# First layer's low weight parts by an adding transfer, with the norm weights moved to the activations

## The chip, the cores and the metric

The kernel runs on one NeuronCore of one Trainium2 chip. The metric is the device time of one execution in microseconds (us); lower is better. Engines are named as in the profile: PE (TensorE matmul) and PEld (its weight loads), DVE (VectorE), ACT (ScalarE), POOL (GpSimd), SP (SyncE, which here only issues transfers).

## What is computed

The reference is a two-layer trunk on a sequence of 512 positions with 1024 features, all in float32:

```python
h = rms_norm(x, norm_g)                       # (512, 1024)
zxbcdt = h @ w_in                             # (1024, 6176): z, x/B/C, dt
xbc = silu(causal_depthwise_conv(xbc, conv_w, conv_b))
y = ssd_chunked_scan(xs * dt, a * dt, bm, cm) + d_skip * xs
y = gated_group_rms_norm(y, z, gate_norm_g)   # silu(z) gate, 8 groups, times g
x = x + y @ w_out                             # (2048, 1024)
k, v = shared_kv(x, kv_norm_g, w_kv)          # second layer: differential attention
x = diff_attention_layer(x, k, v, b_norm_g, b_w_in, ...)
return rms_norm(x, final_norm_g)
```

The first layer is everything up to the second `x =` line. Its two weights are `w_in` and `w_out`; `norm_g` scales the rows of `w_in`, `gate_norm_g` the rows of `w_out`.

## The kernel before

**Split products.** Every dense product is made of three matmuls in the reduced float32 format (float32r). A weight block is split into a high part (the value rounded to float32r) and a low part (what is left), an activation likewise, and `mm3` adds high x high, high x low and low x high into one PSUM bank. So a weight block is of use only when both of its parts are there.

**Segments.** The weights come as a list of segments (`segs`), each 1 MB: 128 partitions x 2048 values. The first layer has 32: `z0_0, z0_1, g0_0, g0_1, g1_0, ...` in the order `z0 g0 g1 z1 g2 g3 z2 g4 o0 g5 z3 g6 g7 o1 o2 o3`, two halves each; `z` and `g` are pieces of `w_in`, `o` of `w_out`. They are numbered 0 to 31 in that order. PE spends 48 matmuls of 512 columns on each.

**Loading and splitting** (`load`, from line 139). One transfer on SP's queue brings the segment into a tile `raw` (two buffers). `split` then makes the tiles `whi` and `wlo` (two buffers each) in four quarters of 128x512: `head` is an ACT instruction that multiplies by the norm weights (one value per partition, `gains`) and rounds; `rest` is a DVE instruction `raw * gain - whi`. Segment 0 is special: its quarters come in four transfers of their own, between those of the transposed input `x_t`, and the first matmuls begin with the first quarter. `split` is a function inside `load` that is called after `load` has returned, and it names its tiles with the variable `i`; in `load(0)` that variable is also the counter of a `for i in range(2, 4)` loop. So the tiles of segment 0 are called `whi3` and `wlo3`.

**What sets the order.** `use(seg)` fetches two segments ahead of the one in use. In the first layer PE's order is the program's; the other engines' instructions are put in order by a scheduler that works with its own estimate of durations, so each engine is a fixed queue once the program is built. POOL makes the decay tiles (`dec`: a subtraction and a masking per head, lines 613 to 616), the state products (`xe`, `hst`) and sums (`dx`). The convolution, the gate and the norm of each group are on DVE and ACT.

**Activations.** `split_x` makes the high part `a_hi` (ACT) and low part `a_lo` (DVE) of the transposed input, without any norm weight; the row factor of the norm comes in later. At the end of each group's scan the normed `y` is transposed into PSUM and split into `yh` and `yl`.

Of the kernel before, what the change touches and what calls it, by code (L numbers as in the profile page):

```python
# [17 lines left out]
P = 128  # L18
# [38 lines left out]
C_GA, C_GK, C_GB, C_GG, C_SG, C_DTB, C_AL, C_CB, C_CW = 0, 8, 16, 24, 40, 41, 42, 43, 75  # L57
# [24 lines left out]
def trunk(ctx, tc, x, x_t, par, w_dt, w_in, w_out, w_kvqg, w_bo, d_skip, lam_qk, fin_g, out):  # L82
    nc = tc.nc
    V, A, T = (Ordered(tc, e) for e in (nc.vector, nc.scalar, nc.tensor))
    GP = nc.gpsimd
# [13 lines left out]
    def ss_bank(name):  # L99
        turns[0] += 1  # L100
        tag = "mm" if turns[0] % turns[1] >= 3 else "ss"
        return psum.tile([P, 512], F32, tag=tag, name=name, bufs=3 if tag == "ss" else 4)
# [8 lines left out]
    segs = []  # L111
# [4 lines left out]
    prm = const.tile([P, C_CB], F32, name="prm")  # L116
# [8 lines left out]
    def source(seg):  # L125
        kind, a, b = seg
        if kind == "z":
            return w_in[a * 6 + b], [prm[:, C_GA + 4 * b + i:C_GA + 4 * b + i + 1] for i in range(4)]
        if kind == "g":
            return w_in[(a // 2) * 6 + 2 + (a % 2) * 2 + b], [prm[:, C_GA + 4 * b + i:C_GA + 4 * b + i + 1] for i in range(4)]  # L130
        if kind == "o":
            return w_out[a * 2 + b], [prm[:, C_GG + 4 * a + i:C_GG + 4 * a + i + 1] for i in range(4)]
        if kind in "bc":
            return w_bo[a], None
        name = f"v{a}" if kind == "v" else a
        at = C_GK if kind in "vk" else C_GB
        ks = range(4 * b, 4 * b + 4) if kind == "v" else range(8)
        return w_kvqg[BLOCKS.index((name, b))], [prm[:, at + i:at + i + 1] for i in ks]
# [5 lines left out]
    def load(i):  # L144

        seg = segs[i]
        src, gains = source(seg)
        nk = 8 if seg[0] in "kqt" else 4
        w = 2048 // nk
        raw = begun[i] if i in begun else wp.tile([P, nk, w], F32, tag="raw", name=f"raw{i}", bufs=2)  # L150
        fetched[0] += 1

        def split():

            pool, tags = (bp, ("dec", "dec")) if seg == ("o", 3, 1) else (wp, ("whi", "wlo"))
            if pool is bp:
                hi, lo = (pool.tile([P, N_DEC], F32R, tag=tag, name=f"{n}{i}", bufs=2)[:, 0:2048].rearrange("p (k n) -> p k n", k=nk)
                          for n, tag in zip(("whi", "wlo"), tags))
            else:
                hi, lo = (pool.tile([P, nk, w], F32R, tag=tag, name=f"{n}{i}", bufs=2) for n, tag in zip(("whi", "wlo"), tags))  # L160
            ready[seg] = (hi, lo)

            def head(k):
                if gains:
                    A.activation(hi[:, k, :], raw[:, k, :], AF.Copy, scale=gains[k])
                else:
                    A.copy(hi[:, k, :], raw[:, k, :])

            def rest(k):
                if gains:  # L170
                    V.scalar_tensor_tensor(out=lo[:, k, :], in0=raw[:, k, :], scalar=gains[k],
                                           in1=hi[:, k, :].bitcast(F32), op0=ALU.mult, op1=ALU.subtract)
                else:
                    V.tensor_tensor(out=lo[:, k, :], in0=raw[:, k, :], in1=hi[:, k, :].bitcast(F32), op=ALU.subtract)

            return [(head, rest, k) for k in range(nk)]

        if i == 0:

            nc.sync.dma_start(raw[:, 0, :], src[:, 0:w])  # L180
            for n in range(2):
                nc.sync.dma_start(xt[0][:, 0, n * 256:(n + 1) * 256], x_t[:, 0, n * 256:(n + 1) * 256])
            nc.sync.dma_start(raw[:, 1, :], src[:, w:2 * w])
            for n in range(2):
                nc.sync.dma_start(xt[0][:, 1, n * 256:(n + 1) * 256], x_t[:, 1, n * 256:(n + 1) * 256])
            for k in range(2, 4):
                nc.sync.dma_start(raw[:, k, :], src[:, k * w:(k + 1) * w])
                nc.sync.dma_start(xt[1][:, k - 2, :], x_t[:, k, :])

            nxt, (src1, _) = wp.tile([P, nk, w], F32, tag="raw", name="raw1", bufs=2), source(segs[1])  # L190
            begun[1] = nxt
            for i in range(2, 4):
                nc.sync.dma_start(xt[i], x_t[:, 2 * i:2 * i + 2, :])
                nc.sync.dma_start(nxt[:, 2 * i - 4:2 * i - 2, :].rearrange("p k n -> p (k n)"), src1[:, (2 * i - 4) * w:(2 * i - 2) * w])
            nc.sync.dma_start(prc[:], par[:, C_CB:N_PAR])
        elif i not in begun:
            nc.sync.dma_start(raw.rearrange("p k n -> p (k n)"), src)
        return split
# [162 lines left out]
    def new_h(tag):  # L361
        return [res.tile([P, KD, S], F32R, tag=f"hT_{i}", name=f"{tag}_{i}") for i in ("hi", "lo")]
# [9 lines left out]
    hh, hl = new_h("a")  # L372
    sctx = ExitStack()
    sm = sctx.enter_context(tc.tile_pool(name="setup", bufs=1))
# [22 lines left out]
    xt = [bp2.tile([P, 2, S], F32, tag="yl", name=f"xt{i}", bufs=4) for i in range(4)]  # L397

    def split_x(k, n=slice(0, S)):
        A.copy(hh[:, k, n], xt[k // 2][:, k % 2, n])  # L400
        V.tensor_tensor(out=hl[:, k, n], in0=xt[k // 2][:, k % 2, n], in1=hh[:, k, n].bitcast(F32), op=ALU.subtract)


    begin = small.tile([P, 1], F32, name="begin", bufs=1)
# [5 lines left out]
    for k in range(4):  # L410
        lay(first[k])
        for n in (slice(0, 256), slice(256, S)) if k < 2 else (slice(0, S),):
            split_x(k, n)
# [5 lines left out]
    for k in range(4, KD):  # L419
        split_x(k)  # L420
# [22 lines left out]
    pre = sm.tile([P, P], F32, name="pre")  # L443
# [4 lines left out]
    e1 = sm.tile([P, P], F32, name="e1")  # L448
# [3 lines left out]
    q1 = sm.tile([P, P], F32, name="q1")  # L452
# [3 lines left out]
    q2 = sm.tile([P, P], F32, name="q2")  # L456
# [3 lines left out]
    for m in (15, 13, 11, 9, 7, 5, 3):  # L460
        V.scalar_tensor_tensor(out=pl, in0=pl, scalar=2.0 / m, in1=q2, op0=ALU.add, op1=ALU.mult)
    V.scalar_tensor_tensor(out=pl, in0=pl, scalar=2.0, in1=q1, op0=ALU.add, op1=ALU.mult)
    dtp = sm.tile([P, P], F32, name="dtp")
    V.scalar_tensor_tensor(out=dtp, in0=pre, scalar=0.0, in1=pl, op0=ALU.max, op1=ALU.add)
    ea = sm.tile([P, 1], F32, name="ea")
    A.activation(ea, prm[:, C_AL:C_AL + 1], AF.Exp)
    adt = sm.tile([P, P], F32, name="adt")
    V.tensor_scalar(out=adt, in0=dtp, scalar1=ea, scalar2=-1.0, op0=ALU.mult, op1=ALU.mult)
    ones = sm.tile([P, P], F32, name="ones")
    GP.memset(ones, 1.0)  # L470
    acs = sm.tile([P, P], F32, name="acs")
    V.tensor_tensor_scan(out=acs, data0=ones, data1=adt, initial=0.0, op0=ALU.mult, op1=ALU.add)
    acs_d = tc.dram_tile([H, NQ, P], F32, name="acs_d")
    for c in range(NQ):
        nc.sync.dma_start(acs_d[:, c, :], acs[c * H:(c + 1) * H, :])
    toe = sm.tile([P, P], F32, name="toe")
    A.activation(toe, acs, AF.Exp, scale=-1.0, bias=acs[:, P - 1:P])
    dsk = const.tile([P, H], F32, name="dsk")
    nc.sync.dma_start(dsk[:], d_skip.partition_broadcast(P))
# [143 lines left out]
    def ssd(g):  # L623
# [7 lines left out]
        for c in range(NQ):  # L631
            cs = slice(c * P, (c + 1) * P)
# [10 lines left out]
        for j in range(2):  # L643
# [6 lines left out]
            with tc.issue_after(next_b.ins) if next_b else ExitStack():  # L650
                V.tensor_tensor(out=xdt[:, :, 2 * j:2 * j + 2, :], in0=pv, in1=dt_tok[:, :, h2].unsqueeze(3).to_broadcast([P, NQ, 2, HD]), op=ALU.mult)
                V.tensor_tensor(out=dx[:, :, 2 * j:2 * j + 2, :], in0=pv,
                                in1=dsk[:, h2].unsqueeze(1).unsqueeze(3).to_broadcast([P, NQ, 2, HD]), op=ALU.mult)
# [42 lines left out]
        for c in (2, 3):  # L696
            T.matmul(po2[:, (c - 2) * 256:(c - 1) * 256], lhsT=cc[:, c * P:(c + 1) * P], rhs=hsf[:, c - 1], start=True, stop=True)
        V.tensor_tensor(out=tmp[:, 1], in0=po1[:, 256:512].rearrange("p (h e) -> p h e", e=HD),
                        in1=eacs_tok[:, 1, hs].unsqueeze(2).to_broadcast([P, R, HD]), op=ALU.mult)
        V.tensor_tensor(out=tmp[:, 2:4], in0=po2.rearrange("p (c h e) -> p c h e", h=R, e=HD),  # L700
                        in1=eacs_tok[:, 2:4, hs].unsqueeze(3).to_broadcast([P, 2, R, HD]), op=ALU.mult)
# [15 lines left out]
        yh = bp2.tile([P, 2, S], F32R, tag="yh", name=f"yh{g}", bufs=4)  # L717
        yl = bp2.tile([P, 2, S], F32R, tag="yl", name=f"yl{g}", bufs=4)
        pyt = [ss_bank(f"pyt{g}_{j}") for j in range(2)]

        n = 2 if g == G - 1 else NQ
        for j, a in [(j, a) for a in range(0, NQ, n) for j in range(2)]:
            if not j:
                yield f"y{a}"
            for c in range(a, a + n):
                T.transpose(pyt[j][:, c * P:(c + 1) * P], tm[:, c, j * P:(j + 1) * P], ident)
            cs = slice(a * P, (a + n) * P)
            A.copy(yh[:, j, cs], pyt[j][:, cs])
            V.tensor_tensor(out=yl[:, j, cs], in0=pyt[j][:, cs], in1=yh[:, j, cs].bitcast(F32), op=ALU.subtract)
        yT[g] = (yh, yl)  # L730

    T.on = True
# [4 lines left out]
    hh, hl = new_h("b")  # L737
# [284 lines left out]
    def half(t, n):  # L1022
        hs = slice(n * 512, (n + 1) * 512)
        return x_tok[:, t, hs], fg[:, hs], ot[t][:, hs], out[t * P:(t + 1) * P, hs]
# [123 lines left out]
    y, f, o, dst = half(3, 0)  # L1148
# [8 lines left out]
    y, f, o, dst = half(3, 1)  # L1157
# [68 lines left out]
```

## Time and profile before

| | |
|---|---|
| median of 3 runs | 708.61 us (708.11 to 708.91) |
| the profiled execution: its own time | 709.16 us |
| its span in the trace | 707.4 us |
| granted TensorE clock, mean over the span | 0.998 |
| busy: PE, PEld | 697.1 us (99%), 579.8 us (82%) |
| busy: DVE, ACT, POOL | 519.5 us (73%), 426.2 us (60%), 113.4 us (16%) |
| read from HBM | 68.02 MB |

The span runs from the first to the last instruction of the trace, and the execution's own time is 1.76 us longer. Busy shares are of the span. The first layer's matmuls run from about 6 us to about 427 us, and what follows is the second layer.

### The profile page before, as it was taken

How to read it: one execution, taken by the hardware profiler on the slowest of the kernel's cores; microseconds unless marked ns; L12 is line 12 of the kernel's file. 1: busy time of each engine (PE TensorE's matmuls, PEld its weight loads, DVE VectorE, ACT ScalarE, POOL GpSimd, SP SyncE). 2: the span in 40 equal slices, each digit the busy share in tenths (PEclk: the TensorE clock that was granted, in tenths of full speed). 3: DMA queues.
4: the chain of work that ended last, by engine and by line, in shares of the span. 5: the costliest groups of instructions: out<-in, count | busy, mean ns of one | idle time of the engine just before them, and what ended most of it. 6: DMA issues, size and time to landing. Idle time of an engine off the chain costs nothing.

```text
span 707.4 us, 10489 instructions
## 1 busy us (share of the span) xinstructions
PE 697.1 (99%) x3838; PEld 579.8 (82%) x3838; DVE 519.5 (73%) x1181; ACT 426.2 (60%) x931; POOL 113.4 (16%) x158
## 2 busy tenths in 40 slices
PE   8999999999999999999999999999999999999996
PEld 7787888887788888888888888888888888888884
DVE  5479975888579669568996846457778657788786
ACT  6748673664653636637636357567777567765556
POOL 0008422402406025041110101000000000000002
PEclk9999999999999999999999999999999999999999
DMA  8643313233033331331122311313112221113003
GB/s 296 253 151 152 120 59 149 91 120 120 38 142 120 100 137 62 111 128 60 60 76 105 120 60 49 136 62 113 67 60 79 86 75 61 68 56 116 31 1 119
DMA packets 13492, 70.85 MB, mean 100 GB/s; under 512 B 1793, under 2 KB 3329, under 8 KB 6017
## 3 DMA queue, kind: packets, MB, share of 16 engines
q1 hardware_dynamic: 13008, 69.90, 27.0%
q8 instruction: 30, 0.49, 0.3%
q10 hardware_dynamic: 432, 0.28, 0.1%
q14 instruction: 22, 0.17, 0.1%
HBM read 68.02 MB, written 2.16 MB: 99 GB/s over the span
## 4 chain that ended last, share of the span: by engine, by line
PE 88%; DVE 4%; DMA 3%; ACT 2%; issue 1%; POOL 1%; SPq 0%; ACTq 0%; POOLq 0%
PE pg L73 23%; PE po L73 16%; PE pt L73 8%; PE pz L73 7%; PE pq L73 6%; PE pk L73 6%; PE pv L73 6%; PE pb L73 3%; DMA raw<-in_w_in 3%; PE sc L73 3%; PE pyd L73 2%; PE pc L73 2%; DVE wlo L73 1%; PE pcb L73 1%; PE psA L73 1%
## 5 line engine op out<-in xcount | busy, mean ns | idle before, releaser
L73 DVE SCALAR_TENSOR_TENSOR wlo<-raw,prm,whi 128x512 fp32r<-128x512 f32 (+1 forms) x240 | 148.7, 669 | 49.2 <-ACT whi L73 47.5
L73 ACT ACTIVATE whi<-raw,prm 128x512 fp32r<-128x512 f32 (+1 forms) x240 | 133.6, 628 | 51.2 <-issue 13.0
L73 PE MATMUL pg<-a_hi,whi 128*128 128x512 f32 x256 | 103.1, 403 | 0.8 <-DVE xc L73 0.4
L73 PE MATMUL pg<-a_hi,wlo 128*128 128x512 f32 x256 | 100.3, 392 | 0.1
L73 PE MATMUL pg<-a_lo,whi 128*128 128x512 f32 x256 | 99.8, 390 | 0.0
L73 DVE SCALAR_TENSOR_TENSOR xc<-pg,prc,xc 128x511 f32<-128x511 f32 (+2 forms) x96 | 69.6, 742 | 6.5 <-ACT xc L73 6.0
L73 PEld LDWEIGHTS pg<-a_hi,wlo 128*128 128x128 f32 x256 | 48.0, 188 | 11.5 <-DVE wlo L73 1.5
L73 PEld LDWEIGHTS pg<-a_hi,whi 128*128 128x128 f32 x256 | 48.1, 188 | 11.2 <-ACT xc L73 0.8
L73 PEld LDWEIGHTS pg<-a_lo,whi 128*128 128x128 f32 x256 | 48.1, 188 | 9.3
L73 PE MATMUL po<-whi,yh 128*128 128x512 f32 x128 | 51.7, 404 | 0.1
L73 PE MATMUL pz<-whi,a_hi 128*128 128x512 f32 x128 | 49.8, 398 | 1.3 <-DVE xc L73 0.7
L73 PE MATMUL po<-whi,yl 128*128 128x512 f32 x128 | 50.1, 391 | 0.0
L73 PE MATMUL po<-wlo,yh 128*128 128x512 f32 x128 | 50.0, 390 | 0.0
L73 PE MATMUL pz<-whi,a_lo 128*128 128x512 f32 x128 | 48.9, 390 | 0.0
L73 PE MATMUL pz<-wlo,a_hi 128*128 128x512 f32 x128 | 48.9, 389 | 0.0
L1031 POOL TENSOR_TENSOR ot<-x_tok,fg 128x512 f32<-128x512 f32 x4 | 5.0, 1284 | 248.9 <-DVE x_tok L73 248.9
L73 ACT ACTIVATE s<-s,mx 128x128 f32<-128x128 f32 (+3 forms) x64 | 35.6, 557 | 10.2 <-DVE mx L73 10.1
L73 DVE CUSTOM_DVE_ANT_0 s<-sc,bias 128x128 f32<-128x128 f32 (+3 forms) x64 | 29.3, 488 | 15.3 <-PE sc L73 14.8
L73 ACT ACTIVATE xc<-pg,prc 128x512 f32<-128x512 f32 x32 | 24.8, 775 | 25.2 <-DVE pg L73 19.6
L656 POOL TENSOR_TENSOR xe<-xdt,tok 128x256 f32<-128x256 f32 x24 | 14.1, 613 | 159.8 <-DVE xdt L73 159.8
L73 ACT ACTIVATE xc<-xc 128x512 f32<-128x512 f32 x32 | 20.0, 629 | 28.0 <-DVE xc L73 24.1
L73 ACT ACT_TABLE_LOAD x23 | 29.5, 1283 | 10.2 <-DVE xc L73 8.7
(238 smaller groups left out, 1629.8 us busy)
## 6 DMA issues: line engine op xcount, KB each, us to landing
raw<-in_w_in SPq DMA_DIRECT2D x22, 1024.0 KB, 4.9
raw<-in_w_kvqg SPq DMA_DIRECT2D x16, 1024.0 KB, 4.8
dec<-acs_d SPq DMA_DIRECT2D x8, 1024.0 KB, 5.4
raw<-in_w_out SPq DMA_DIRECT2D x8, 1024.0 KB, 4.8
raw<-in_w_bo SPq DMA_DIRECT2D x4, 1024.0 KB, 4.8
x_tok<-in_x SPq DMA_DIRECT2D x4, 512.0 KB, 8.9
out<-ot SPq DMA_DIRECT2D x6, 256.0 KB, 2.1
raw<-in_w_in SPq DMA_DIRECT2D x4, 256.0 KB, 5.0
```

Source lines behind the costliest of these rows:

```text
L73: i = op(*args, **kw)
L656: GP.tensor_tensor(out=xe[:, c], in0=xdt[:, c], in1=toe_tok[:, c, hs].unsqueeze(2).to_broadcast([P, R, HD]), op=ALU.mult)
L1031: GP.tensor_tensor(out=o, in0=y, in1=f, op=ALU.mult)
```

## The change

- For the segments of the first layer whose index satisfies a condition (`added`, below), `rest` is no longer a DVE instruction. POOL writes `-whi` into `wlo`, quarter by quarter, and after the fourth quarter POOL issues one transfer that reads the whole segment from HBM a second time and adds it onto `wlo`.
- The norm weights of the first layer leave the weights: `head` is a plain rounding copy there, `split_x` multiplies the input by `norm_g`, and the split of `y` multiplies by `gate_norm_g`, each in the same instruction as before.
- `whi` and `wlo` have three buffers instead of two. To make room, four small tiles of the setup share others' space (`dtp` is `pre`, `adt` is `q2`, `acs` is `e1`, `toe` is `q1`), and the space for descriptors of POOL's transfers is set to 1024 bytes.

```diff
-            return w_in[a * 6 + b], [prm[:, C_GA + 4 * b + i:C_GA + 4 * b + i + 1] for i in range(4)]
+            return w_in[a * 6 + b], None
...
+            added = seg[0] in "zgo" and 1 < i < segs.index(("o", 3, 0))
...
-                hi, lo = (pool.tile([P, nk, w], F32R, tag=tag, name=f"{n}{i}", bufs=2) for n, tag in zip(("whi", "wlo"), tags))
+                hi, lo = (pool.tile([P, nk, w], F32R, tag=tag, name=f"{n}{i}", bufs=3) for n, tag in zip(("whi", "wlo"), tags))
...
             def rest(k):
-                if gains:
+                if added:
+                    GP.tensor_scalar(out=lo[:, k, :], in0=hi[:, k, :].bitcast(F32), scalar1=-1.0, scalar2=None, op0=ALU.mult)
+                    if k == nk - 1:
+                        GP.dma_start(lo.rearrange("p k n -> p (k n)"), src, accum_op=ALU.add)
+                elif gains:
...
     def split_x(k, n=slice(0, S)):
-        A.copy(hh[:, k, n], xt[k // 2][:, k % 2, n])
-        V.tensor_tensor(out=hl[:, k, n], in0=xt[k // 2][:, k % 2, n], in1=hh[:, k, n].bitcast(F32), op=ALU.subtract)
+        ga = prm[:, C_GA + k:C_GA + k + 1]
+        A.activation(hh[:, k, n], xt[k // 2][:, k % 2, n], AF.Copy, scale=ga)
+        V.scalar_tensor_tensor(out=hl[:, k, n], in0=xt[k // 2][:, k % 2, n], scalar=ga, in1=hh[:, k, n].bitcast(F32),
+                               op0=ALU.mult, op1=ALU.subtract)
...
-            A.copy(yh[:, j, cs], pyt[j][:, cs])
-            V.tensor_tensor(out=yl[:, j, cs], in0=pyt[j][:, cs], in1=yh[:, j, cs].bitcast(F32), op=ALU.subtract)
+            gg = prm[:, C_GG + 2 * g + j:C_GG + 2 * g + j + 1]
+            A.activation(yh[:, j, cs], pyt[j][:, cs], AF.Copy, scale=gg)
+            V.scalar_tensor_tensor(out=yl[:, j, cs], in0=pyt[j][:, cs], scalar=gg, in1=yh[:, j, cs].bitcast(F32),
+                                   op0=ALU.mult, op1=ALU.subtract)
```

The condition reads `i` when `split` runs. For segment 0 that value is 3, left there by the loop in `load(0)`, so `added` holds for segment 0 too; it does not hold for segment 1 nor for 30 and 31. In all, 29 segments are concerned.

POOL's queue at the start of the program, before. `ident` is the unit matrix for transposes, `adiag` belongs to the input's norm, `dec0` and `dec1` are the decay tiles of the first two groups:

```order
masks.py:199 AFFINE_SELECT ident_74<-ident_74 128x128
L337 MEMSET adiag_253 128x128
L339 TENSOR_TENSOR adiag_253<-ident_74,ar_col_239 128x128 x4
L613 COPY dec0_543<-dec0_543 128x8
L615 TENSOR_TENSOR dec0_543<-dec0_543,tok_434 128x512 x4
L616 AFFINE_SELECT dec0_543<-dec0_543 128x512 x2
L613 COPY dec1_562<-dec1_562 128x8
L616 AFFINE_SELECT dec0_543<-dec0_543 128x512 x2
L615 TENSOR_TENSOR dec1_562<-dec1_562,tok_434 128x512 x4
```

The same place now, where `wlo3_134` is the low part of segment 0:

```order
masks.py:199 AFFINE_SELECT ident_74<-ident_74 128x128
L172 TENSOR_SCALAR wlo3_134<-whi3_133 128x512 x4
L174 DMA wlo3_134<-in_w_in 128x2048
L342 MEMSET adiag_254 128x128
L344 TENSOR_TENSOR adiag_254<-ident_74,ar_col_240 128x128 x4
L172 TENSOR_SCALAR wlo2_346<-whi2_345 128x512 x4
L174 DMA wlo2_346<-in_w_in 128x2048
L172 TENSOR_SCALAR wlo3_359<-whi3_358 128x512 x4
L174 DMA wlo3_359<-in_w_in 128x2048
L172 TENSOR_SCALAR wlo4_438<-whi4_437 128x512 x4
```

The low part of segment 0 is now four negations and one transfer of the whole 1 MB at the head of this queue.

PE's queue at the same place, before. The `pz0` banks take the products of segment 0:

```order
L73 MATMUL pz0_2_137<-whi3_133,a_hi_80 128x512
L73 MATMUL pz0_3_138<-whi3_133,a_hi_80 128x512
L73 MATMUL pz0_0_135<-wlo3_134,a_hi_80 128x512
L73 MATMUL pz0_1_136<-wlo3_134,a_hi_80 128x512
L73 MATMUL pz0_2_137<-wlo3_134,a_hi_80 128x512
```

And now:

```order
L73 MATMUL pz0_2_137<-whi3_133,a_hi_80 128x512
L73 MATMUL pz0_3_138<-whi3_133,a_hi_80 128x512
L73 MATMUL pz0_0_135<-wlo3_134,a_hi_80 128x512
L73 MATMUL pz0_0_135<-whi3_133,a_lo_81 128x512
L73 MATMUL pz0_1_136<-wlo3_134,a_hi_80 128x512
```

In both, the fifth matmul of segment 0 is the first that reads the low part, and 43 more of that segment stand behind it.

POOL's queue a little later, now. `wlo5_503` is the low part of segment 5, the second half of `g1`; the `dec` work is the same as before the change, in another place:

```order
L620 COPY dec0_544<-dec0_544 128x8
L620 COPY dec1_563<-dec1_563 128x8
L174 DMA wlo4_438<-in_w_in 128x2048
L172 TENSOR_SCALAR wlo5_503<-whi5_502 128x512 x4
L622 TENSOR_TENSOR dec0_544<-dec0_544,tok_433 128x512 x4
L622 TENSOR_TENSOR dec1_563<-dec1_563,tok_433 128x512 x4
L174 DMA wlo5_503<-in_w_in 128x2048
```

The transfer of segment 5 stands behind both groups' eight subtractions, which need `tok` from DVE.

More of the change, by code (lines that the diff above doesn't have):

```diff
@@ L127, in source @@
         if kind == "z":
-            return w_in[a * 6 + b], [prm[:, C_GA + 4 * b + i:C_GA + 4 * b + i + 1] for i in range(4)]
+            return w_in[a * 6 + b], None
         if kind == "g":
-            return w_in[(a // 2) * 6 + 2 + (a % 2) * 2 + b], [prm[:, C_GA + 4 * b + i:C_GA + 4 * b + i + 1] for i in range(4)]
+            return w_in[(a // 2) * 6 + 2 + (a % 2) * 2 + b], None
         if kind == "o":
-            return w_out[a * 2 + b], [prm[:, C_GG + 4 * a + i:C_GG + 4 * a + i + 1] for i in range(4)]
+            return w_out[a * 2 + b], None
         if kind in "bc":
@@ L462, in trunk @@
     V.scalar_tensor_tensor(out=pl, in0=pl, scalar=2.0, in1=q1, op0=ALU.add, op1=ALU.mult)
-    dtp = sm.tile([P, P], F32, name="dtp")
+    dtp = pre
     V.scalar_tensor_tensor(out=dtp, in0=pre, scalar=0.0, in1=pl, op0=ALU.max, op1=ALU.add)
@@ L466, in trunk @@
     A.activation(ea, prm[:, C_AL:C_AL + 1], AF.Exp)
-    adt = sm.tile([P, P], F32, name="adt")
+    adt = q2
     V.tensor_scalar(out=adt, in0=dtp, scalar1=ea, scalar2=-1.0, op0=ALU.mult, op1=ALU.mult)
@@ L470, in trunk @@
     GP.memset(ones, 1.0)
-    acs = sm.tile([P, P], F32, name="acs")
+    acs = e1
     V.tensor_tensor_scan(out=acs, data0=ones, data1=adt, initial=0.0, op0=ALU.mult, op1=ALU.add)
@@ L475, in trunk @@
         nc.sync.dma_start(acs_d[:, c, :], acs[c * H:(c + 1) * H, :])
-    toe = sm.tile([P, P], F32, name="toe")
+    toe = q1
     A.activation(toe, acs, AF.Exp, scale=-1.0, bias=acs[:, P - 1:P])
@@ L1218 @@
     arrays = {f"in_{k}": np.ascontiguousarray(v) for k, v in arrays.items()}
-    nc = bacc.Bacc("TRN2", target_bir_lowering=False, num_devices=1)
+    nc = bacc.Bacc("TRN2", target_bir_lowering=False, num_devices=1, dynamic_dma_scratch_size=1024)
     args = [nc.dram_tensor(k, v.shape, mybir.dt.from_np(v.dtype), kind="ExternalInput").ap() for k, v in arrays.items()]
```

## The prediction

> **What bounds the kernel now.** I read the page's first part, then what PE's weight loads waited for, then the timeline of the first 34 us. The page first:
>
> ```profile
> span 707.4 us, 10489 instructions
> PE 697.1 (99%) x3838; PEld 579.8 (82%) x3838; DVE 519.5 (73%) x1181; ACT 426.2 (60%) x931; POOL 113.4 (16%) x158
> q1 hardware_dynamic: 13008, 69.90, 27.0%
> ```
>
> PE is busy for 697.1 of 707.4 us, and the change neither adds nor removes a matmul. What it can win is time in which PE waits. The view of waits, for the weight loads (which show a stall before the busy share of PE does; columns: us in total, times, longest):
>
> ```profile
> PEld pz L73 <- ACT xc L73: 1.6, 2, 1.1
> PEld pg L73 <- DVE wlo L73: 1.5, 5, 0.6
> PEld pz L73 <- ACT a_hi L73: 0.9, 1, 0.9
> PEld pg L73 <- ACT xc L73: 0.8, 1, 0.8
> PEld ps_dt L73 <- DVE wlo L73: 0.8, 1, 0.8
> PEld pg L73 <- ACT zs L73: 0.7, 1, 0.7
> PEld po L73 <- ACT xc L73: 0.5, 1, 0.5
> PEld pyt L73 <- DVE yl L73: 0.4, 1, 0.4
> PEld pg L73 <- ACT whi L73: 0.4, 1, 0.4
> ```
>
> These are the first layer's, 7.6 us together. Only 1.5 + 0.8 + 0.4 = 2.7 us of it is for weight parts. So DVE, from which the change takes the most work, is hardly ever what PE waits for.
>
> **What it takes off, and what that is worth.** The groups and the tile view of `raw`:
>
> ```profile
> L73 DVE SCALAR_TENSOR_TENSOR wlo<-raw,prm,whi 128x512 fp32r<-128x512 f32 (+1 forms) x240 | 148.7, 669 | 49.2 <-ACT whi L73 47.5
> L73 ACT CAST whi<-raw x16: 602/616/623, 613.7 to 674.0; 128x512 fp32r<-128x512 f32 x16
> L73 ACT ACTIVATE whi<-raw,prm x240: 492/707/761, 4.6 to 632.5; 128x512 fp32r<-128x512 f32 x72, 128x256 fp32r<-128x256 f32 x48
> ```
>
> 29 segments x 4 quarters = 116 DVE instructions of about 0.7 us go: some 80 us of DVE time, beside PE's work. ACT's 128 roundings of the first layer go from 0.71 to 0.62 us, 12 us less, also beside it. The scaled splits of input and `y` replace unscaled ones one for one, about 0.1 us more each on ACT by the same two rows; at the start they fit into ACT's waits for transfers, later they are a few tenths: nothing. The worth on PE is a share of the 7.6 us: between 0 and 7.6, and I take 3, the weight parts' own 2.7 and a little of the convolution's.
>
> **The start.** `added` holds for segment 0, and the fifth matmul of PE's queue reads its low part. Rows of the timeline (start, duration), and two groups (the number behind the bar and comma is the mean length in ns):
>
> ```profile
> 1.47 3.89 PE L73 MATMUL warm<-ident 128*128 128x128 f32 x17 [1.47 <-POOL ident masks.py:199]
> 6.84 1.08 PE L73 MATMUL pz<-wlo,a_hi 128*128 128x512 f32 x4
> 10.94 0.72 ACT L73 ACTIVATE whi<-raw,prm 128x512 fp32r<-128x512 f32 x1 [0.78 <-DMA raw<-in_w_in]
> 16.82 0.39 PE L73 MATMUL pz<-whi,a_hi 128*128 128x512 f32 x1
> 16.79 13.33 SPq L197 DMA_DIRECT2D raw<-in_w_in  x3
> 26.27 2.56 ACT L73 ACTIVATE whi<-raw,prm 128x512 fp32r<-128x512 f32 x4 [2.98 <-DMA raw<-in_w_in]
> 665.47 0.60 PE L73 MATMUL pt<-ident,s 128*128 128x128 f32 x4
> ...
> L73 PE MATMUL warm<-ident 128*128 128x128 f32 x17 | 3.9, 421 | 1.5 <-POOL ident masks.py:199 1.5
> L73 PE MATMUL pt<-ident,s 128*128 128x128 f32 x80 | 14.0, 273 | 0.1
> ```
>
> Before, PE reads the first quarter of the low part at 6.84 us and begins segment 1 at 16.82: 44 matmuls in 9.98 us, 0.227 us each, without a gap. Now all four quarters come with one transfer, which can't be issued before the fourth quarter of `whi` is there. PE's queue is fixed and stands at its fifth matmul until that transfer lands at a time T; every us of T beyond 6.84 is lost, since behind it the same 44 matmuls take the same 9.98 us.
>
> T in steps. The fourth quarter of `whi` is bound by its transfer and ends at 10.94 + 0.62 = 11.6. POOL then negates the last quarter and issues the transfer. Neither is in the trace; the nearest rows are POOL's masking and subtraction of 128x512 tiles, and an issue on SP:
>
> ```profile
> 57.03 1.23 POOL L616 TENSOR_SCALAR_AFFINE_SELECT dec<-dec 128x512 f32<-128x512 f32 x2
> 53.00 4.08 POOL L615 TENSOR_TENSOR dec<-dec,tok 128x512 f32<-128x512 f32 x4
> 60.00 5.41 POOL L615 TENSOR_TENSOR dec<-dec,tok 128x512 f32<-128x512 f32 x4
> 204.63 0.33 SPq L197 DMA_DIRECT2D raw<-in_w_in  x1
> ```
>
> A negation lies between 0.62 and 1.35 us; I take 0.7, near the one-input row. The issue lies between SP's 0.33 and a POOL instruction's 1.02; I take 1.0, as POOL's is not SP's kind. That gives 13.3. The transfer itself: the plain 1 MB loads and the load on the engines at that time:
>
> ```profile
> raw<-in_w_in SPq DMA_DIRECT2D x22, 1024.0 KB, 4.9
> 14.00:26.00 12.00, 12.00 (x55) 9.94 (x54) 7.07 (x20) 8.40 (x15) 0.57 (x3) 1.00 1.00 402
> ```
>
> A plain load takes 4.9 us in the median, but from 14 to 26 us the transfer engines are full (share 1.00, 402 GB/s), and the load issued at 16.79 is awaited until 26.27: 9.4 us. An accumulation also has to read what it adds to, and no row shows one. Its bounds are 4.9 and 2 x 9.4 = 18.8; I take 9.4, the row of the same size in the same crowd. So T = 13.3 + 9.4 = 22.7 (18.2 to 32.1), and PE loses 15.9 us (11.4 to 25.3).
>
> The row with which one can differ is the 9.4: the page shows one busy queue, q1, so that load stood behind the earlier ones of its own queue. [...] No run here shows two full queues side by side.
>
> After some 16 idle us PE starts slowly. In the rows above the first 17 transposes after the start stand 0.217 us apart ((3.89 - 0.42) / 16, with 0.42 for the last one's length), later ones 0.110 ((0.60 - 0.27) / 3). If the restart costs what the first start does, 3.89 us run at half pace: 2.0 us lost, and 0 at the least. [...]
> **The second half of g1.** Let S be the start of `g0` on PE. Before the transfer of segment 5, POOL has to do the eight subtractions, which need `tok`; that is made 22 steps of three matmuls into `g0`: S + 22 x 0.68 = S + 15, with transposes and DVE's copy S + 16. By the rows above the subtractions take 4.08 + 5.41 = 9.5, the issue 1.0: S + 26.5. At this time the engines have room, so the transfer takes between 4.9 and twice that, 9.8; I take 7. It lands at S + 33.5. PE has done `g0` (32 steps, 21.8 us, and the transposes) and the 8 steps of `g1` that need only segment 4 (`TURNS`) at S + 27.7. Stall: 6 us (3.7 to 8.6).
>
> **The other segments.** The third buffer lets `whi` of segment n be made when PE is done with n - 3, two segments ahead. From that moment rounding takes 2.6 us, the last negation 0.7, the issue 1.0, the transfer 4.9 to 9.8: 9.2 to 14.1 us, against two segments of PE work, 2 x 10.9. In most places that is enough. It is tight where POOL's queue has put the transfer of segment n behind the negation of n + 1 and PE has no scan work in between (second halves of `g4` and `g5`: about 11.3 us of PE work), or behind `dx` sums and the decay tile (second halves of `g3` and `g7`). For each of the four I set 0 to 3 us and take 1.
>
> **Sum.** 15.9 + 2.0 + 6 + 4 - 3 = 24.9 us more. The profiled execution's own time was 709.16 (span 707.4); on the median of 708.61 it is 733.5. The low end of all terms: 11.4 + 0 + 3.7 + 0 - 7.6 = 7.5, or 716.1; the high end: 25.3 + 2.0 + 8.6 + 2.0 for a second slow restart + 12 - 0 = 49.9, or 758.5.
>
> **Rivals.** *The transfer is far slower than two loads.* If an accumulation passes its bytes three times (two reads and a write), 3 x 4.9 = 14.7 us outside the crowd and, say, 19 in it, then T is 32 and the start loses 25.3 + 2.0, `g1` 13.5, and the four tight places about 6.5 each, 26: 67 - 3 = 64 us more, 773. It decides from about 12 us per transfer on. For it: no row excludes it; against it: between the loads the engines are idle (q1 uses 27.0% of them). Chance 0.13.
>
> *Segment 0 keeps DVE's path.* The text of `added` reads like "all but the first two"; if it did so, the start would be as before, and the sum would be 6 + 4 - 3 = 7 us, 715.6. The order of the built program speaks against it: the transfer into `wlo3` is POOL's first. Chance 0.02.
>
> *Faster.* PE's waits in the first layer go, since DVE has 80 us less to do, and no transfer is late: 708.61 - 7.6 = 701.0. For this the low part of segment 0 would have to land by 6.84 us, or PE have other work until then; it can't be issued before 11.6, and PE's queue has four matmuls ahead of it. Chance 0.03 for any gain over 0.2%.
>
> **Numbers.** The forecast, slower by a stall at the start and smaller ones after it, has 0.80. The range goes from 716 (the low end) to 764, a little beyond the high end towards the slow transfer: that leaves out most of the first rival and the few cases below. 0.2% of 708.6 is 1.4 us, about what a measurement of this kernel can tell from none: slower 0.95, within it 0.02, faster 0.03.
>
> **What would show it.** In the changed kernel's profile PE should stand idle from about 7 us to 20 to 32 us, released by POOL's transfer into `wlo`, with a lower granted clock just after; segment 1 should begin about 18 us later than 16.82; a wait of `pg` on a transfer should stand at the second half of `g1`; DVE's busy time should be near 440 us; and from the end of the first layer on all should be as before, shifted. I am wrong if PE does not wait at its fifth matmul, if later stalls outweigh the start, or if the accumulation takes under 5 us in the crowd.

## The result and the profile after

The changed kernel takes 768.34 us (median of 4 runs, 766.14 to 769.4) beside 708.42 us (708.11 to 708.91) of the kernel before in the same session. The ratio is 1.0841 with a 95% interval of 1.0813 to 1.0869: slower by 8.4%, about 60 us. The forecast was 733.5 us, with a range from 716 to 764. The sign was right and the size was not.

The page of the changed kernel, its first part, queues, chain, largest POOL group and two DMA issues:

```profile
span 767.5 us, 10541 instructions
PE 714.4 (93%) x3838; PEld 590.5 (77%) x3838; DVE 467.0 (61%) x1065; ACT 418.0 (54%) x931; POOL 300.6 (39%) x303
q1 hardware_dynamic: 13008, 69.90, 24.7%
q0 software_dynamic: 4176, 30.41, 21.3%
PE 69%; DMA 10%; POOL 8%; DVE 6%; ACT 3%; issue 2%; SPq 0%; ACTq 0%; POOLq 0%; DVEq 0%
L172 POOL TENSOR_SCALAR wlo<-whi 128x512 fp32r<-128x512 f32 x116 | 172.9, 1543 | 56.5 <-ACT whi L73 56.5
...
wlo<-in_w_in POOLq DMA_DIRECT2D x23, 1024.0 KB, 9.0
dec<-acs_d SPq DMA_DIRECT2D x8, 1024.0 KB, 8.3
```

PE has the same 3838 matmuls, but its share has fallen from 99% to 93%: span less busy time is now 53.1 us, and it was 10.3. So 42.8 of the 60 us are plain idle time. The other 17.3 us stand in PE's busy time (714.4 after 697.1). Nearly all of it are matmuls just after a stall: the granted clock is 0.50 in eight stretches of the first layer, the last one ending at 411.4, and in them PE is busy for 32 us in all. At half pace (a matmul every 0.43 us instead of 0.23) that costs about 16 us (the first of these stretches is shown under the start). DVE gave up 52.5 us that PE hardly waited for, and POOL took on 187.2. Of the chain that ended last PE had 88% before and has 69% now; DMA has 10% and POOL 8% of it, after 3% and 1%. The 116 negations are POOL's largest group: 172.9 us, or 1.49 us each when divided by their count (the mean of 1543 ns counts overlaps). An adding transfer takes 9.0 us in the median, a plain one of the same size 4.9 as before.

The view of waits says where the idle time lies (us in total, times, longest):

```profile
PE pz L73 <- DMA wlo<-in_w_in: 18.3, 1, 18.3
PE pg L73 <- DMA wlo<-in_w_in: 15.0, 5, 5.8
PE psA L73 <- POOL xe L663: 4.4, 2, 2.7
PE pg L73 <- DVE xc L73: 2.7, 1, 2.7
PE psB L73 <- POOL xe L663: 2.7, 2, 1.3
PE pxt L73 <- DVE yl L73: 1.7, 1, 1.7
```

One long wait at the start, five shorter ones on the low parts, and four (7.1 us) that have nothing to do with a weight: there PE waits for `xe`, a state product of the scan that POOL makes. Two more are for `xc` and `yl`, which DVE makes.

To see when the time is lost, I read the start of the same step on PE in both traces. The lag of the changed kernel at six such steps, in us (the first number is the step's time before):

| step on PE | before, at | after | 0 on DVE | only 0 | none | on ACT | ACT, 0 on DVE | no transfer | POOL subtracts | fixed order |
|---|---|---|---|---|---|---|---|---|---|---|
| `ps_tt`, in `g0` | 46.1 | +19.8 | +21.1 | +18.9 | -0.4 | +18.3 | +14.2 | -0.6 | +0.6 | +16.4 |
| `pyd`, scan of the 1st group | 74.7 | +29.0 | +29.2 | +21.0 | -1.2 | +17.5 | +14.3 | +9.3 | +2.8 | +24.9 |
| `pcb`, 3rd | 144.0 | +36.3 | +34.8 | +21.2 | -1.2 | +22.8 | +18.6 | +13.2 | +7.2 | +46.9 |
| `pyd`, 4th | 213.6 | +49.9 | +47.7 | +19.5 | -2.9 | +25.3 | +25.0 | +16.7 | +8.9 | +54.1 |
| `pyd`, 6th | 305.6 | +50.5 | +48.3 | +19.5 | -2.9 | +25.3 | +25.0 | +17.2 | +9.2 | +64.4 |
| `btp`, second layer | 433.7 | +60.4 | +58.0 | +19.2 | -3.2 | +32.4 | +30.0 | +23.3 | +13.2 | +82.9 |

The last eight columns are the experiments below. In the column after, a third is lost at the start (19.8), 9.3 up to the first group's scan, and 31.3 in the rest of the first layer; from there on everything is shifted by 60.

**The start.** POOL's and PE's timelines of the changed kernel (start, duration; in brackets the idle time before and its releaser):

```profile
11.14 1.49 POOL L172 TENSOR_SCALAR wlo<-whi 128x512 fp32r<-128x512 f32 x1 [0.92 <-ACT whi L73]
12.95 1.04 POOL L174 DMA_DIRECT2D wlo<-in_w_in  x1 [0.33 <-POOL wlo L172]
```

```profile
25.04 0.77 PE L73 MATMUL pz<-wlo,a_hi 128*128 128x512 f32 x1 [18.26 <-DMA wlo<-in_w_in]
25.60 0.63 PE L73 MATMUL pz<-whi,a_lo 128*128 128x512 f32 x1
26.03 0.63 PE L73 MATMUL pz<-wlo,a_hi 128*128 128x512 f32 x1
...
29.78 0.39 PE L73 MATMUL pz<-wlo,a_hi 128*128 128x512 f32 x1
30.01 0.39 PE L73 MATMUL pz<-whi,a_lo 128*128 128x512 f32 x1
```

PE does four matmuls and stands at the fifth until 25.04, 18.2 us later than before (6.84). The fifth matmul starts 12.1 us after the transfer's issue at 12.95. Then matmuls follow each other at 0.43 us until about 29, and at 0.23 after that. The windows show the granted clock (last three columns: clock, DMA share, GB/s):

```profile
10.00:20.00 10.00, 0.00 (x0) 0.00 (x0) 6.09 (x10) 7.33 (x12) 2.75 (x3) 0.50 1.05 365
20.00:30.00 10.00, 4.96 (x13) 3.96 (x14) 2.25 (x12) 4.19 (x8) 0.33 (x2) 0.54 1.01 358
30.00:40.00 10.00, 10.00 (x99) 7.82 (x98) 0.00 (x0) 4.11 (x8) 9.69 (x11) 1.00 0.50 148
```

**Later.** Three places on POOL, and what PE does then:

```profile
71.06 8.40 POOL L622 TENSOR_TENSOR dec<-dec,tok 128x512 f32<-128x512 f32 x8
79.12 1.22 POOL L174 DMA_DIRECT2D wlo<-in_w_in  x1
...
196.28 4.40 POOL L172 TENSOR_SCALAR wlo<-whi 128x512 fp32r<-128x512 f32 x3 [2.43 <-ACT whi L73]
200.66 1.18 POOL L663 TENSOR_TENSOR xe<-xdt,tok 128x256 f32<-128x256 f32 x2
201.82 1.48 POOL L172 TENSOR_SCALAR wlo<-whi 128x512 fp32r<-128x512 f32 x1
...
228.69 11.72 POOL L172 TENSOR_SCALAR wlo<-whi 128x512 fp32r<-128x512 f32 x8 [3.98 <-ACT whi L73]
240.35 0.89 POOL L174 DMA_DIRECT2D wlo<-in_w_in  x1
```

```profile
87.57 0.76 PE L73 MATMUL pg<-a_hi,wlo 128*128 128x512 f32 x1 [3.50 <-DMA wlo<-in_w_in]
201.32 1.27 PE L73 MATMUL psA<-xe,bt 128*128 128x256 f32 x4 [1.70 <-POOL xe L663]
203.94 1.22 PE L73 MATMUL psB<-xe,bt 128*128 128x256 f32 x2 [1.34 <-POOL xe L663]
248.53 0.76 PE L73 MATMUL pg<-a_hi,wlo 128*128 128x512 f32 x1 [5.80 <-DMA wlo<-in_w_in]
```

At 87.57 the transfer stood behind the eight subtractions of the decay tile. At 201 and 204 the state products stood behind three negations and then one more. At 248.53 eight negations, of two segments, stood ahead of one transfer: 11.7 us before its issue could begin.

The wait of 2.7 us for `xc`, at 171.79, has POOL behind it too, in another way:

```profile
164.96 6.02 DVE L73 TENSOR_TENSOR dx<-dx,zs 128x256 f32<-128x256 f32 x2
```

The first of these two DVE instructions took 5.69 us, where the median of all 32 is 0.43. It ended at 170.65, just after POOL had gone through four subtractions and a masking of the decay tile without a break (165.46 to 170.36). In this trace nine DVE instructions took at least 0.7 us longer than the shortest of their kind, 21.6 us together, each while POOL worked on the decay tile; before the change there are four, 3.2 us together. Three of the nine, of a kind that takes 0.15 us, took 0.97 to 0.98 us while one of POOL's subtractions ran (from 328.16, 329.16 and 330.17). So a long run of POOL's work on the decay tile held up DVE as well. What ties the two engines together, no run here isolates.

### The profile page after: what moved, and what is told of

It is laid out like the page before. It is cut to its first block, busy times and chain, and to the rows that moved or that the text cites. A ratio compares the mean times of both kernels' runs of the same rounds, so it can differ in the third digit from the quotient of the medians.

```text
span 767.5 us, 10541 instructions
## 1 busy us (share of the span) xinstructions
PE 714.4 (93%) x3838; PEld 590.5 (77%) x3838; DVE 467.0 (61%) x1065; ACT 418.0 (54%) x931; POOL 300.6 (39%) x303
## 3 DMA queue, kind: packets, MB, share of 16 engines
q1 hardware_dynamic: 13008, 69.90, 24.7%
q0 software_dynamic: 4176, 30.41, 21.3%
## 4 chain that ended last, share of the span: by engine, by line
PE 69%; DMA 10%; POOL 8%; DVE 6%; ACT 3%; issue 2%; SPq 0%; ACTq 0%; POOLq 0%; DVEq 0%
PE pg L73 15%; PE po L73 15%; PE pt L73 7%; POOL wlo L172 6%; DMA wlo<-in_w_in 6%; PE pq L73 6%; PE pk L73 6%; PE pv L73 6%; PE pb L73 3%; PE pz L73 3%; PE sc L73 3%; DMA dec<-acs_d 2%; PE pc L73 2%; PE pyd L73 2%; DVE dx L73 1%
## 5 line engine op out<-in xcount | busy, mean ns | idle before, releaser
L172 POOL TENSOR_SCALAR wlo<-whi 128x512 fp32r<-128x512 f32 x116 | 172.9, 1543 | 56.5 <-ACT whi L73 56.5
L73 PE MATMUL pg<-a_hi,wlo 128*128 128x512 f32 x256 | 103.7, 405 | 15.0 <-DMA wlo<-in_w_in 15.0
L73 ACT CAST whi<-raw 128x512 fp32r<-128x512 f32 x144 | 78.8, 617 | 59.0 <-PE pg L73 27.6
L73 PE MATMUL pg<-a_hi,whi 128*128 128x512 f32 x256 | 105.7, 413 | 2.7 <-DVE xc L73 2.7
L73 PE MATMUL pg<-a_lo,whi 128*128 128x512 f32 x256 | 102.2, 399 | 0.0
L73 PEld LDWEIGHTS pg<-a_hi,wlo 128*128 128x128 f32 x256 | 49.8, 194 | 27.9 <-issue 6.4
L73 PE MATMUL pz<-wlo,a_hi 128*128 128x512 f32 x128 | 51.2, 400 | 18.3 <-DMA wlo<-in_w_in 18.3
L73 DVE SCALAR_TENSOR_TENSOR wlo<-raw,prm,whi 128x256 fp32r<-128x256 f32 (+1 forms) x112 | 51.8, 519 | 19.3 <-ACT whi L73 19.2
L73 ACT ACTIVATE whi<-raw,prm 128x256 fp32r<-128x256 f32 (+1 forms) x112 | 50.9, 530 | 20.0 <-PE po L73 7.6
L73 DVE TENSOR_TENSOR pg<-pg,ar_row 128x512 f32<-128x512 f32 x32 | 22.2, 695 | 51.4 <-PE pg L73 51.3
L73 PEld LDWEIGHTS pz<-wlo,a_hi 128*128 128x128 f32 x128 | 24.9, 194 | 23.6 <-issue 18.7
```

The costliest lines, as they stand in the source:

```text
L73: i = op(*args, **kw)
L172: GP.tensor_scalar(out=lo[:, k, :], in0=hi[:, k, :].bitcast(F32), scalar1=-1.0, scalar2=None, op0=ALU.mult)
```

## The experiments

The edits are given against the changed kernel. The theory: each low part now comes some 11 to 14 us after its last rounding (1.49 + 0.33 + 9.0 = 10.8 from the rows above, 13.9 at the start), where PE has no other work, and POOL's negations hold up the transfers and the scan's own steps behind them. The rivals: the start alone explains it; the transfers alone do; or the moved norm weights and the third buffer cost something themselves. The scheduler orders the queues anew for each edit, so a run can differ from its neighbour by more than the lines shown.

**Segment 0 back on DVE** (column "0 on DVE").

```diff
-            added = seg[0] in "zgo" and 1 < i < segs.index(("o", 3, 0))
+            added = seg[0] in "zgo" and 1 < segs.index(seg) < segs.index(("o", 3, 0))
```

> The changed kernel with the condition read from the segment's own number, so that segment 0 keeps DVE's path; nothing else is changed. Theory A (the start is one separate loss: 18.3 us of waiting at PE's fifth matmul and 2 us of slow restart, 20 in all): 748, with no wait of PE before 40 us and the lags at g1 and after it as in the changed kernel. Rival B (the later lateness is set by POOL and the transfers, and a late start only hides it): the time regained at the start comes back as longer later stalls, 755 to 768.

Measured: 768.06 us (766.84 to 769.6), ratio 1.0843 (1.0825 to 1.086), no different from the changed kernel, as Rival B expected. The start is as it was before the change, and the wait has moved. POOL and PE around segment 2, now the first one made by a transfer:

```profile
27.15 16.04 POOL L172 TENSOR_SCALAR wlo<-whi 128x512 fp32r<-128x512 f32 x11
43.15 0.96 POOL L174 DMA_DIRECT2D wlo<-in_w_in  x1
```

```profile
51.25 0.76 PE L73 MATMUL pg<-a_hi,wlo 128*128 128x512 f32 x1 [19.85 <-DMA wlo<-in_w_in]
```

Eleven negations, of three segments, stand in POOL's queue ahead of segment 2's transfer. So the loss is not bound to segment 0 and its crowded start, and the 20 us of the start can't be had back by exempting that segment alone.

**Only segment 0 by the transfer** (column "only 0").

```diff
-            added = seg[0] in "zgo" and 1 < i < segs.index(("o", 3, 0))
+            added = seg == ("z", 0, 0)
```

> The changed kernel with the transfer for segment 0 alone; all other low parts are made by DVE from the unscaled weights. Theory A: 708.5 + 20 = 728.5, with one wait of about 18 us at PE's fifth matmul. If the norm weights on the activations or the third buffer cost anything by themselves, it is above 731; if what comes after can take up part of the late start, below 726.

Measured: 730.62 us (728.03 to 733.01), ratio 1.0312 (1.028 to 1.0344). PE waits 17.1 us at its fifth matmul, and from the first step of the table on the lag stays between 19 and 21. At the first step the start alone costs 18.9 us, near the 17.9 (15.9 + 2.0) of its terms in the prediction. The whole kernel is 22 us slower than before (20 to 25 in its four runs): the 3 us of gain do not show here, and one new wait of 2.7 us stands at 87.70. The loss is not additive with the rest, as the run above shows.

**No low part by the transfer** (column "none"); what is left of the change are the moved norm weights, the third buffer and the shared setup tiles.

```diff
-            added = seg[0] in "zgo" and 1 < i < segs.index(("o", 3, 0))
+            added = False
```

> The changed kernel without any adding transfer: the norm weights on the activations, three buffers and the shared setup tiles alone. Theory A (all of the loss comes from POOL's negations and transfers): 705 to 709, the third buffer taking away part of the 7.6 us of waits of before. Rival C (the moved norm weights or the shared tiles cost time of their own, on ACT or by new waits between setup tiles): 711 or more.

Measured: 705.74 us (705.55 to 707.67), ratio 0.9971 (0.9958 to 0.9984): faster than the kernel before. PE's matmuls have no wait left but that for the first warm-up. Of the waits of its weight loads, `pg` for `wlo` (1.5 us before) is no longer listed, and `pz` for `xc` has gone from 1.6 to 0.7 us:

```profile
PEld ps_dt L73 <- DVE wlo L73: 0.8, 1, 0.8
PEld pz L73 <- ACT xc L73: 0.7, 2, 0.5
```

This is within Theory A's 705 to 709. So everything that is lost comes from the negations and transfers, and the rest of the change wins about 2.5 us.

**Negations on ACT** (column "on ACT"). POOL keeps only the issues.

```diff
-                    GP.tensor_scalar(out=lo[:, k, :], in0=hi[:, k, :].bitcast(F32), scalar1=-1.0, scalar2=None, op0=ALU.mult)
+                    A.activation(lo[:, k, :], hi[:, k, :].bitcast(F32), AF.Copy, scale=-1.0)
```

> The changed kernel with the 116 negations on ACT (0.62 us each by its roundings) instead of POOL (1.49 us each); the transfers stay on POOL, segment 0 among them. Theory A (after the start, POOL's queue is what makes low parts and state products late, as four negations hold it for 5.9 us per segment): the start keeps about 19 us, of the 40 after it 10 or less are left: 732 to 740. Rival D (a transfer of 9 us after the rounding is late by itself, whoever negates): 752 to 762.

Measured: 741.18 us (736.79 to 741.72), ratio 1.0444 (1.0409 to 1.0479): 27 us less than the changed kernel, just above Theory A's range and well below Rival D's. ACT's group, and PE's waits:

```profile
L73 ACT ACTIVATE wlo<-whi 128x512 fp32r<-128x512 f32 x116 | 66.6, 623 | 0.1
```

```profile
PE pz L73 <- DMA wlo<-in_w_in: 15.9, 1, 15.9
PE pg L73 <- DMA wlo<-in_w_in: 7.5, 3, 3.5
```

The same 116 negations take 66.6 us on ACT, 0.62 each. The waits for `xe` are gone, and so is the whole loss between the first two steps of the table. With the transfers only, and 66.6 us more work on ACT, 18.3 us are lost at the start and 14 later. Counted by the order of the transfers, the three waits of `pg` are at the second halves of `g3`, `g4` and `g7` (1.50, 2.45 and 3.54 us).

**Negations on ACT, segment 0 on DVE** (column "ACT, 0 on DVE"): both edits above together.

```diff
-            added = seg[0] in "zgo" and 1 < i < segs.index(("o", 3, 0))
+            added = seg[0] in "zgo" and 1 < segs.index(seg) < segs.index(("o", 3, 0))
-                    GP.tensor_scalar(out=lo[:, k, :], in0=hi[:, k, :].bitcast(F32), scalar1=-1.0, scalar2=None, op0=ALU.mult)
+                    A.activation(lo[:, k, :], hi[:, k, :].bitcast(F32), AF.Copy, scale=-1.0)
```

> Negations on ACT, and segment 0 on DVE's path; the transfers of segments 2 to 29 stay. Segment 2 arrives at 26.3 us; rounding and negation 5 us, issue 1, transfer 8: its low part is there at about 40, and PE wants it at 31. Theory E (a low part comes 14 us or more after its segment, so that the first one that is made so stops PE, whichever it is): a wait of about 9 us at segment 2 and the 15 us of lateness after the start that were there with segment 0's transfer: 730 to 736. Rival F (only POOL's queue order made segment 2 late): no wait there, 721 to 726.

Measured: 738.44 us (736.95 to 739.37), ratio 1.0415 (1.0399 to 1.0432). Segment 2 on POOL and PE:

```profile
34.35 1.01 POOL L174 DMA_DIRECT2D wlo<-in_w_in  x1 [6.06 <-ACT wlo L73]
```

```profile
43.78 0.76 PE L73 MATMUL pg<-a_hi,wlo 128*128 128x512 f32 x1 [11.76 <-ACT wlo L73]
```

The row names ACT as releaser, but ACT had released POOL's issue 9.4 us earlier; PE waited for the transfer. Rival F, without a wait here, is refuted; Theory E had the place right, but the wait is 11.8 us instead of 9 and the time is above its range. Exempting segment 0 saves 2.7 us between the medians, and the ranges overlap: the first segment that comes by a transfer stops PE, even with a cheap negation and an issue 8.8 us earlier.

**No transfer** (column "no transfer"): POOL negates, and `wlo` is left at that, so the low part leaves out the weights.

```diff
-                    if k == nk - 1:
-                        GP.dma_start(lo.rearrange("p k n -> p (k n)"), src, accum_op=ALU.add)
```

> The changed kernel without the adding transfers: POOL writes the negated high part as the low part, and PE reads that (so the low part leaves out the weights themselves). What stays is POOL's 5.9 us per segment. Theory E (two costs: POOL's negations, and the 9 us of each transfer behind them): the start loses about 6 us (last negation at 12.6 instead of the first low quarter at 6.84), segment 2 about 2, the late state products about 8: 718 to 726. If the transfers make all the lateness after the start, 710 to 714; if the negations make it, 735 or more.

Measured: 732.43 us (731.76 to 733.68), ratio 1.0335 (1.0319 to 1.035), above the 718 to 726 of Theory E and below the 735 from which on the negations would make all the lateness. Nothing is lost at the start. PE's wait for the state products, and a longer one in its timeline:

```profile
PE psA L73 <- POOL xe L661: 8.5, 2, 4.6
```

```profile
83.97 3.62 PE L73 MATMUL pyd<-xdt,dec 128*64 128x64 f32 x64 [9.84 <-issue]
```

The last row gives its wait no releaser. The tile `dec` that `pyd` reads comes from POOL's subtractions and maskings, then ACT's exponential, then a product on DVE:

```profile
56.24 5.86 POOL L172 TENSOR_SCALAR wlo<-whi 128x512 fp32r<-128x512 f32 x4
62.07 8.11 POOL L620 TENSOR_TENSOR dec<-dec,tok 128x512 f32<-128x512 f32 x8
70.13 1.22 POOL L621 TENSOR_SCALAR_AFFINE_SELECT dec<-dec 128x512 f32<-128x512 f32 x2
...
73.03 1.22 POOL L621 TENSOR_SCALAR_AFFINE_SELECT dec<-dec 128x512 f32<-128x512 f32 x2
...
81.38 2.48 DVE L73 TENSOR_TENSOR dec<-dec,pcb 128x512 f32<-128x512 f32 x4 [4.24 <-ACT dec L73]
```

The subtractions stand behind negations, and the first group's four maskings end at 74.25, 13.8 us later than in the version with none (60.43). ACT's exponential starts at 79.44, behind instructions of the convolution in its own queue, and DVE's product ends at 83.86, when `pyd` can start.

So POOL's negations cost 26 us against the version with none, with no transfer at all, by making the scan's decay tile and state products late. How much of it the new order of ACT's queue adds, no run separates.

**POOL subtracts, no transfer** (column "POOL subtracts"): the low part as `raw - whi` directly.

```diff
-                    GP.tensor_scalar(out=lo[:, k, :], in0=hi[:, k, :].bitcast(F32), scalar1=-1.0, scalar2=None, op0=ALU.mult)
-                    if k == nk - 1:
-                        GP.dma_start(lo.rearrange("p k n -> p (k n)"), src, accum_op=ALU.add)
+                    GP.tensor_tensor(out=lo[:, k, :], in0=raw[:, k, :], in1=hi[:, k, :].bitcast(F32), op=ALU.subtract)
```

> The changed kernel with the low part made by one subtraction on POOL (raw less high part) and no transfer; all else as changed. It asks what a POOL instruction with a float32r result costs, as the subtraction with a float32 result takes 1.02 us and the negation 1.49. If the result's type is what is slow, each takes 1.5 us or more and the time is that of the kernel without transfers, 718 to 728; if the form of the negation (one input and a constant) is slow, each takes 1.0 to 1.3 us and the time is 712 to 717.

Measured: 721.93 us (721.58 to 722.95), ratio 1.0187 (1.017 to 1.0204). POOL's groups:

```profile
L172 POOL TENSOR_TENSOR wlo<-raw,whi 128x512 fp32r<-128x512 f32 x116 | 147.6, 1303 | 75.4 <-ACT whi L73 75.4
L620 POOL TENSOR_TENSOR dec<-dec,tok 128x512 f32<-128x512 f32 x32 | 34.1, 1095 | 0.2
L621 POOL TENSOR_SCALAR_AFFINE_SELECT dec<-dec 128x512 f32<-128x512 f32 x32 | 19.6, 641 | 0.0
```

The subtraction of two tiles takes 1.27 us (147.6 by 116), the negation of one 1.49. The neighbouring subtraction with a plain float32 result takes 1.07. Of the two expectations the duration fits the second (1.0 to 1.3 us) and the time the first (718 to 728). No run has the negation with a float32 result, so it stays open how much of its 1.49 us is the result type and how much the operation. Being 0.2 us shorter 116 times, it costs 10.5 us less than the negations without a transfer. POOL could have made the whole low part in less time than it took to negate `whi`, though DVE, with room to spare, does that better (705.74 us in the version without the transfer).

**A fixed order on POOL** (column "fixed order"): segment 0 on DVE, and the scheduler keeps negations and transfers in program order.

```diff
-            added = seg[0] in "zgo" and 1 < i < segs.index(("o", 3, 0))
+            added = seg[0] in "zgo" and 1 < segs.index(seg) < segs.index(("o", 3, 0))
-                    GP.tensor_scalar(out=lo[:, k, :], in0=hi[:, k, :].bitcast(F32), scalar1=-1.0, scalar2=None, op0=ALU.mult)
+                    tc.keep_in_program_order(GP.tensor_scalar(out=lo[:, k, :], in0=hi[:, k, :].bitcast(F32), scalar1=-1.0, scalar2=None, op0=ALU.mult))
-                        GP.dma_start(lo.rearrange("p k n -> p (k n)"), src, accum_op=ALU.add)
+                        tc.keep_in_program_order(GP.dma_start(lo.rearrange("p k n -> p (k n)"), src, accum_op=ALU.add))
```

> Segment 0 on DVE's path, negations on POOL, and the negations and transfers kept in the order in which the program writes them, so that the transfer of segment 2 stands right behind its own negations and not behind those of 3 and 4. Theory E: negations of segment 2 end at 33, its transfer lands at 42, PE wants it at 31: 12 us lost there instead of 20, the rest nearly as with the condition mended alone: 755 to 762. Rival F (the order is the whole loss at segment 2): 745 to 750.

Measured: 792.77 us (790.38 to 794.41), ratio 1.1181 (1.1155 to 1.1207), outside what was expected. Segment 2 on POOL and PE, and PE's waits:

```profile
32.61 1.04 POOL L174 DMA_DIRECT2D wlo<-in_w_in  x1 [0.33 <-POOL wlo L172]
```

```profile
45.64 0.76 PE L73 MATMUL pg<-a_hi,wlo 128*128 128x512 f32 x1 [14.47 <-DMA wlo<-in_w_in]
```

```profile
PE pg L73 <- DMA wlo<-in_w_in: 64.2, 6, 14.6
```

The transfer is issued 10.5 us earlier than with 11 negations ahead of it, but PE's wait only falls from 19.9 to 14.5 us: from issue to PE's matmul it is 13.0 us here (45.64 - 32.61) and 8.1 there (51.25 - 43.15). And the fixed order makes later segments wait, 49.8 us in five more waits. The scheduler's mix was not the cause of the loss; it kept it smaller.

**The gain apart**: no low part by the transfer, with two buffers as before, and with three once more.

```diff
-            added = seg[0] in "zgo" and 1 < i < segs.index(("o", 3, 0))
+            added = False
-                hi, lo = (pool.tile([P, nk, w], F32R, tag=tag, name=f"{n}{i}", bufs=3) for n, tag in zip(("whi", "wlo"), tags))
+                hi, lo = (pool.tile([P, nk, w], F32R, tag=tag, name=f"{n}{i}", bufs=2) for n, tag in zip(("whi", "wlo"), tags))
```

> The norm weights on the activations alone, with two buffers of whi and wlo and no transfer. If the third buffer brought the 2.7 us that the variant with three buffers gained on the kernel before, this one is at 708 to 709; if the cheaper roundings on ACT (0.62 instead of 0.71 us) brought it, at 705 to 707.

> The variant without transfers and with three buffers again, on the same chip as the one with two buffers, for a closer interval: 705 to 707, ratio 0.996 to 0.998 to the kernel before.

Measured: 706.85 us (705.92 to 707.51), ratio 0.9959 (0.9925 to 0.9992), with two buffers; 706.13 us (705.84 to 707.55), ratio 0.9969 (0.9956 to 0.9981), with three. The first is in the range expected if the cheaper roundings bring the gain, the second in its own; the medians are 1.6 and 2.3 us below that of the kernel before (708.42). The two can't be told apart, so the third buffer is not shown to add anything. With the moved norm weights ACT's roundings take 0.62 us, and PE's short waits for `wlo` are gone or nearly so. Three buffers without the transfer, at 705.74 and 706.13 us, has the lowest medians here, 0.3% under the kernel before.

## Why the prediction was wrong

**What bounds the kernel: right.** PE with 7.6 us of first-layer waits to win, so nothing that DVE gives up could be worth much. DVE's busy time was forecast near 440 us and is 467.0; the nine DVE instructions that POOL held up account for 21.6 us of it, and with the negations on ACT it is 445.2. The "about 0.7 us" of one DVE instruction was a mean over two sizes; those of 128x512 took 0.75.

**The start: right in size, with two of its parts off.** The 44 matmuls from the fifth to the next step took 12.0 us instead of 9.98, so the slow restart cost the 2.0 us of the sum: the granted clock was 0.50 from 8.7 to 29.1 us, in the idle time and in the first matmuls after it. The wait cost 18.2 instead of 15.9: the last negation ended at 12.63 (1.49 us, not 0.7) and PE went on 12.1 us after the issue began, where the sum had 1.0 + 9.4. T itself, 25.0, lies within its bounds. Outside the full start an adding transfer is slow too: 9.0 us in the median of 23, where a plain one of the same size takes 4.9.

**The second half of `g1`: right place, 9.3 instead of 6.** There are two waits, not one: segment 4's transfer was late too (3.11 us at 76.77). POOL had negated that segment by 57.69, but in its queue the transfer stands behind two copies into `dec`, which waited until 64.29 for transfers of their own. Segment 5's transfer was issued at 79.12, behind the eight subtractions as foreseen. After each of them the next matmuls again follow at 0.43 us instead of 0.23, which adds most of the other 2.7 us.

**"The other segments": this is the step that failed.** I set 0 to 3 us for each of four tight places and took 1, 4 us in all; the runs show 31.3. Over this stretch (74.7 to 433.7 us before, 103.7 to 494.0 after) PE's idle time went from 1.1 to 20.2 us, of which 8.3 are waits for low parts, 7.0 for `xe` and 4.7 for DVE, and its busy time grew by 12.2. Three things were wrong with the step.

First, the negation was "near the one-input row" of 0.7 us and is 1.49. So a segment keeps POOL for 6 us instead of 2.8, and two segments' negations ahead of one transfer cost 11.7 us before its issue (5.80 us lost at 248.53, and 2.19 us in the same way at 362.16). I had kept 1.35 us as the upper end, and 1.49 lies beyond it. With 116 instructions this term was the one to bound most carefully. Of the four places only the second half of `g4` stopped PE for its low part; the 2.19 us are at the second half of `g6`. With the negations off POOL, PE waits at three of the four places, 7.5 us in all: these places were well chosen for the transfers, and priced too low.

Second, the sum held POOL only as the way to the transfer. It left out POOL's other customers, the decay tile and the state products, for which PE waits as well, and DVE, which POOL held up.

Third, the sum had one slow restart (two at the high end). In this stretch alone the granted clock is 0.50 five more times, with 21.8 us of busy PE, so about 11 us are lost by that.

The table splits the 31.3 us. Between the same two steps the run with the negations on ACT loses 14.9 us, the run without any transfer 14.0, and the version without low parts by the transfer gains 2.0. Over the whole kernel POOL's negations cost 26 us (732.43 against 706.1), and the transfers, with the added work on ACT, 35 us (741.18 against 706.1). Together that is 61 of the 62 us between the changed kernel and the version without its low parts. I don't claim that they add up in general: the two runs that exempt segment 0 show that a loss avoided at one place comes back at the next.

**The gain: right, and swallowed.** I took 3 us for the waits that go; the version without the transfer is 2.3 to 2.6 us faster than before.

**The rivals.** The slow transfer gave 773 us, near the measured time, but it is not what happened. It needed 14.7 us per transfer outside the crowd and decided from 12; the median is 9.0. The time agrees by another sum, in which 26 us come from POOL's negations. That segment 0 keeps DVE's path is refuted by the wait at the fifth matmul; had it done so, the time would not have been 715.6 but 768.06, as the run with that edit shows. The faster rival needed a low part that lands by 6.84 us; it landed at 25. Of what I said would make me wrong, one thing came true: the later stalls (40.6 us) outweigh the start (19.8).

## What to carry to other kernels

Before work moves to a lightly loaded engine, list who waits for what that engine already does: its 16% busy share says nothing about the steps that PE needs from it at once. A busy engine directly behind the producer (here DVE, 0.7 us after the rounding) can be better than a chain of idle ones that takes 11 us or more. Where a stage moves as a whole onto a longer path, exempting its first piece may save nothing, since the next piece then becomes the first.

## What the runs showed of the hardware

- On POOL a multiplication of one 128x512 tile by a constant, with a float32r result, took 1.49 us; a subtraction of two such tiles 1.27 with the same result type; a masking with a float32 result 0.61 (19.6 by 32). ACT took 0.62 for the same negation. DVE's own subtraction of two such tiles took 0.69 before the change.
- A transfer that adds onto SBUF took 8.6 to 9.0 us for 1 MB in the median and some 12 in the full start, a plain one 4.8 to 4.9. Its queue q0 used 21.3% of the transfer engines for 30.41 MB, where q1 used 24.7% for 69.90: about twice the time per byte. The plain `dec` transfers beside it went from 5.4 to 8.3 us.
- Issuing a transfer kept POOL itself for about 1 us, and 0.3 to 0.4 us passed between its own last negation and the issue behind it.
- DVE instructions took up to 5.69 us instead of 0.43 while POOL subtracted and masked the decay tile without a break.
- PE's 512-column matmuls started 0.43 us apart at a granted clock of 0.50 and 0.23 at 1.00. In the changed kernel each of the seven waits from 2.2 to 18.3 us was followed by a stretch at 0.50; in the run with the negations on ACT one of 2.66 us was not (0.23 us between the next matmuls).
